# A gated linear unit over 268 MB: two load buffers and two product buffers replaced by three slots with the product packed in place

## The chip, the cores and the metric

The kernel runs on one core of one Trainium2 chip. The metric is the device time of one execution in microseconds (us); lower is better. The time that a run reports is about 2 us more than the span of its profile (936.0 against 933.9 for the profiled run of the kernel before).

## The reference

```python
def setup_inputs():
    return {"x": np.random.randn(8192, 8192).astype(np.float32)}

def reference(x):
    a, b = np.split(x, 2, axis=-1)
    return a * (1 / (1 + np.exp(-b)))
```

Each row of 8192 numbers is cut into halves a and b, and a · sigmoid(b), 4096 numbers, goes out. 268.4 MB are read and 134.2 MB written, all in float32.

## The kernel before

The 8192 rows are cut into 32 tiles. A tile has 128 partitions with two rows each, so 64 KiB per partition come in (one contiguous piece) and 32 KiB go out. SyncE issues the loads, ScalarE does the sigmoid in place and issues the stores, VectorE multiplies into a second tile. Both tiles have two buffers: 2 x (64 + 32) = 192 KiB per partition. (In the cuts of code below, `...` marks what is left out, and some comments after `#` are mine.)

```python
pool = ctx.enter_context(tc.tile_pool(name="io", bufs=2))
for i in range(n_tiles):
    x_sb = pool.tile([P, R * n_cols], fp32)
    o_sb = pool.tile([P, R * half], fp32)
    load = nc.sync.dma_start(out=x_sb, in_=x_t[i])
    ...
    n = 4 if i == n_tiles - 1 else 1        # the last tile in eight small pieces
    w = half // n
    for r in range(R):                      # R = 2 rows
        for c in range(n):
            ...
            nc.scalar.activation(out=b, in_=b, func=SIG)
            nc.vector.tensor_mul(out=o_sb[:, cols], in0=a, in1=b)
            if n > 1:
                nc.scalar.dma_start(out=out_t[i, :, cols], in_=o_sb[:, cols])
    if n == 1:
        nc.scalar.dma_start(out=out_t[i], in_=o_sb)
```

After scheduling, ScalarE's instruction list is, for every tile but the last: two activations, then that tile's store. At the end of the build the first load is moved up into the entry block.

## Time and profile before

| | before |
|---|---|
| median of 6 runs | 936.12 us (935.98 to 937.0) |
| span of the profile | 933.9 us |
| VectorE, ScalarE busy | 280.9, 230.0 us |
| two DMA queues' packets, share of 16 engines' span | 66.5% + 33.3% |

The page's busy shares, queue totals and chain, and the stretches of time, are shown in the prediction below. Two more views matter later. The first is the issue queue of SyncE, which issues the loads (what waited, for what: us in total, times, longest):

```profile
SPq L28 <- DMA x_sb<-in_x_dram: 482.8, 30, 20.8
SPq L28 <- DVE o_sb L39: 374.3, 30, 12.8
```

A load waits for an earlier load (that of its buffer, two tiles back) and then for the product that frees the buffer. It never waits for a store. The second is the page's list of DMA issues (count, KB each, us from issue to landing, the median):

```profile
out_dram<-o_sb ACTq DMA_DIRECT2D x31, 4096.0 KB, 41.7
x_sb<-in_x_dram SPq DMA_DIRECT2D x32, 45.5
```

### The profile page before, as it was taken

The numbers are of one execution on the slowest core, as the hardware profiler recorded it, in microseconds if no ns is written. First come the engines' busy times: TensorE is split into PE (matmuls) and PEld (weight loads), VectorE is DVE, ScalarE is ACT, GpSimd is POOL, SyncE is SP. The second block draws the span as 40 slices with busy tenths as digits, with TensorE's granted clock in tenths as the row PEclk, the third lists the DMA queues.
The fourth block names the chain that finished last, engine by engine and source line by source line (L and its number), as shares of the span: only waits on it lengthen the run. The fifth ranks groups of instructions, "written<-read, shape, count | busy, mean of one in ns | idle before, by whom it ended". The sixth has DMA issues, their size and how long they took to land.

```text
span 933.9 us, 410 instructions
## 1 busy us (share of the span) xinstructions
DVE 280.9 (30%) x70; ACT 230.0 (25%) x71; POOL 0.2 (0%) x4
## 2 busy tenths in 40 slices
DVE  0333321333213333133331333312333123331234
ACT  1313331133311333203332033320233202333023
POOL 0000000000000000000000000000000000000000
DMA  9999999999999999999999999999999999999998
GB/s 404 420 434 431 453 418 429 439 434 449 420 456 404 452 424 427 449 425 451 412 459 410 438 438 425 451 421 452 413 449 421 431 445 443 429 420 453 410 446 362
DMA packets 10226, 402.67 MB, mean 431 GB/s; under 512 B 1136, under 2 KB 1136, under 8 KB 2160
## 3 DMA queue, kind: packets, MB, share of 16 engines
q1 hardware_dynamic: 4608, 268.44, 66.5%
q10 hardware_dynamic: 5616, 134.22, 33.3%
q14 instruction: 2, 0.02, 0.0%
HBM read 268.44 MB, written 134.22 MB: 431 GB/s over the span
## 4 chain that ended last, share of the span: by engine, by line
DMA 78%; DVE 15%; ACT 6%; issue 0%; DVEq 0%; ACTq 0%
DMA x_sb<-in_x_dram 78%; DVE o_sb L39 15%; ACT x_sb L38 6%; DVEq L61 0%; ACTq L41 0%; ACTq L38 0%
## 5 line engine op out<-in xcount | busy, mean ns | idle before, releaser
L39 DVE TENSOR_TENSOR o_sb<-x_sb 128x4096 f32<-128x4096 f32 (+1 forms) x70 | 280.9, 4056 | 647.2 <-ACT x_sb L38 647.2
L38 ACT ACTIVATE x_sb<-x_sb 128x4096 f32<-128x4096 f32 (+1 forms) x70 | 228.7, 3315 | 695.9 <-DMA x_sb<-in_x_dram 691.8
L38 ACT ACT_TABLE_LOAD x1 | 1.3, 1283 | 0.8 <-PEq L85 0.8
L85 POOL MEMSET const-uint8-127<- 128x1 uint8 x1 | 0.1, 103 | 0.0
L85 POOL MEMSET const-bfloat16-1.0<- 128x1 bf16 x1 | 0.1, 102 | 0.0
L85 POOL MEMSET const-float32-0.0<- 128x1 f32 x1 | 0.1, 99 | 0.2 <-issue 0.2
L85 POOL MEMSET const-float32-1.0<- 128x1 f32 x1 | 0.1, 99 | 0.0
## 6 DMA issues: line engine op xcount, KB each, us to landing
out_dram<-o_sb ACTq DMA_DIRECT2D x31, 4096.0 KB, 41.7
out_dram<-o_sb ACTq DMA_DIRECT2D x8, 512.0 KB, 6.2
x_sb<-in_x_dram SPq DMA_DIRECT2D x32, 45.5
```

The lines of the kernel that those rows point to most:

```text
L38: nc.scalar.activation(out=b, in_=b, func=SIG)
L39: nc.vector.tensor_mul(out=o_sb[:, cols], in0=a, in1=b)
L85: nc = _bacc.Bacc("TRN2", target_bir_lowering=False, num_devices=1)
```

## The change

Its intent: use the same 192 KiB as three slots, so that three loads can be under way; write the product into the first half of its own slot; do one activation and one product per tile; and declare away waits that follow from others, so that each instruction keeps one. (`tc.keep_in_program_order` stops the scheduler from moving an instruction in its engine's list.) The core of the diff (blank lines and unchanged parts cut):

```diff
-    pool = ctx.enter_context(tc.tile_pool(name="io", bufs=2))
+    SLOTS = 3
+    pool = ctx.enter_context(tc.tile_pool(name="slots", bufs=1))
+    slots = [pool.tile([P, R * n_cols], fp32, name=f"slot{k}") for k in range(SLOTS)]
+    def implied(later, *earlier):
+        for e in earlier:
+            tc.declare_no_dep(later.ins, e.ins, reason="follows from the wait that is kept")
...
+        rows = slot.rearrange("p (r h m) -> p r h m", r=R, h=2)
+        packed = slot[:, : R * half].rearrange("p (r m) -> p r m", r=R)
+        def load(cols):
+            ins = nc.sync.dma_start(out=slot[:, cols], in_=x_t[i, :, cols])
+            implied(ins, *(e for e in gone if e not in awaited))   # keeps the slot's last stores
...
+        def glu(r, c):
+            sig = nc.scalar.activation(out=rows[:, r, 1, c], in_=rows[:, r, 1, c], func=SIG)
+            mul = nc.vector.tensor_mul(
+                out=packed[:, r, c], in0=rows[:, r, 0, c], in1=rows[:, r, 1, c]
+            )
...
+            if i == n_tiles - 1:
+                tc.keep_in_program_order(sig)
...
+        def store(cols):
+            ins = nc.scalar.dma_start(out=out_t[i, :, cols], in_=slot[:, cols])
...
+        if i < n_tiles - 1:
+            load(slice(0, R * n_cols))
+            glu(slice(0, R), every)
+            n_stores = R if i == n_tiles - 2 else 1
+            w = R * half // n_stores
+            for k in range(n_stores):
+                store(slice(k * w, (k + 1) * w))
+        else:
+            for r in range(R):
+                load(slice(r * n_cols, (r + 1) * n_cols))
+            for r in range(R):
+                halves = [slice(0, half // 2), slice(half // 2, half)]
+                for c in [every] if r == 0 else halves:
+                    glu(slice(r, r + 1), c)
+                store(slice(r * half, (r + 1) * half))
```

The diff doesn't show one thing. Here is how ScalarE's instruction list compares, as built (A n is the activation of tile n, S n its store):

```
before : A0 A0 S0  A1 A1 S1  A2 A2 S2  A3 A3 S3  A4 A4 S4  ...
changed: A0 S0  A1 S1  A2 S2  A3 A4 S3 S4  A5 S5  A6 A7 S6 S7  A8 S8  ... A27 A28 S27 S28 ...
```

From tile 3 on the scheduler puts every third tile's store behind the next tile's activation, nine times in all.

More of the change, by code (lines that the diff above doesn't have):

```diff
@@ L20, in _tiles @@
     out_t = out.rearrange("(n p r) m -> n p (r m)", p=P, r=R)
-    pool = ctx.enter_context(tc.tile_pool(name="io", bufs=2))
-    first = None
-    for i in range(n_tiles):
-        x_sb = pool.tile([P, R * n_cols], fp32)
-        o_sb = pool.tile([P, R * half], fp32)
-        load = nc.sync.dma_start(out=x_sb, in_=x_t[i])
-        first = first or load
-        n = 4 if i == n_tiles - 1 else 1
-        w = half // n
-        for r in range(R):
-            for c in range(n):
-                lo = r * n_cols + c * w
-                a = x_sb[:, lo : lo + w]
-                b = x_sb[:, lo + half : lo + half + w]
-                cols = slice(r * half + c * w, r * half + (c + 1) * w)
-                nc.scalar.activation(out=b, in_=b, func=SIG)
-                nc.vector.tensor_mul(out=o_sb[:, cols], in0=a, in1=b)
-                if n > 1:
-                    nc.scalar.dma_start(out=out_t[i, :, cols], in_=o_sb[:, cols])
-        if n == 1:
-            nc.scalar.dma_start(out=out_t[i], in_=o_sb)
@@ L44, in _tiles @@
-    return first
+    pool = ctx.enter_context(tc.tile_pool(name="slots", bufs=1))
[3 more added lines that the diff above has]
+            tc.declare_no_dep(later.ins, e.ins, reason="follows from the wait that is kept")
+    kinds = ("loads", "sigs", "muls", "stores")
+    history = [{k: [] for k in kinds} for _ in range(SLOTS)]
+    last_stores = [[] for _ in range(SLOTS)]
+    every = slice(0, half)
@@ new lines, in _tiles @@
+    for i in range(n_tiles):
+        slot = slots[i % SLOTS]
+        old = history[i % SLOTS]
+        now = {k: [] for k in kinds}
+        gone = sum(old.values(), [])
+        awaited = last_stores[i % SLOTS]
+        rows = slot.rearrange("p (r h m) -> p r h m", r=R, h=2)
[3 more added lines that the diff above has]
+            implied(ins, *(e for e in gone if e not in awaited))
+            now["loads"].append(ins)
+        def glu(r, c):
[3 more added lines that the diff above has]
+            )
+            implied(sig, *gone)
+            implied(mul, *gone, *now["loads"])
+            if i == n_tiles - 1:
+                tc.keep_in_program_order(sig)
+            now["sigs"].append(sig)
+            now["muls"].append(mul)
+        def store(cols):
+            ins = nc.scalar.dma_start(out=out_t[i, :, cols], in_=slot[:, cols])
+            implied(ins, *(e for e in gone if e not in old["stores"]), *now["loads"], *now["sigs"])
+            now["stores"].append(ins)
+        if i < n_tiles - 1:
[13 more added lines that the diff above has]
+                store(slice(r * half, (r + 1) * half))
+        for k in kinds:
+            old[k] += now[k]
+        last_stores[i % SLOTS] = now["stores"]
@@ L64 @@
     SP = mybir.EngineType.SP
-    at = next(k for k, i in enumerate(body) if i.engine == SP)
+    at = next(k for k, i in enumerate(body) if i.engine == SP and i.opcode == "DMACopy")
     load = body[at]
```

## The prediction

> **What bounds the kernel now.** I read the page from its top (busy shares, slices, DMA queues), then its chain of waits, then stretches of time with their DMA share, then the issue queue's waits, and last single packet records.
>
> ```profile
> span 933.9 us, 410 instructions
> DVE 280.9 (30%) x70; ACT 230.0 (25%) x71; POOL 0.2 (0%) x4
> DMA  9999999999999999999999999999999999999998
> q1 hardware_dynamic: 4608, 268.44, 66.5%
> q10 hardware_dynamic: 5616, 134.22, 33.3%
> HBM read 268.44 MB, written 134.22 MB: 431 GB/s over the span
> DMA 78%; DVE 15%; ACT 6%; issue 0%; DVEq 0%; ACTq 0%
> ```
>
> The two queues' packets (q1 loads, q10 stores) take 66.5% + 33.3% = 99.8% of the time of the 16 DMA engines: 932 of 933.9 us. VectorE and ScalarE are at 30% and 25%. All 402.7 MB have to cross and the change leaves that number alone. The chain of waits seems to say otherwise: it gives 15% to VectorE and 6% to ScalarE. Here is how that chain looks in order of time (start, us, what), for one pair of tiles:
>
> ```profile
> 811.23 45.45 DMA x_sb<-in_x_dram
> 856.67 0.02 issue
> 856.70 0.02 ACTq L38
> 856.71 0.04 issue
> 856.76 3.62 ACT x_sb L38
> 860.38 0.02 issue
> 860.41 8.77 DVE o_sb L39 x2
> 869.18 0.02 issue
> 869.19 45.42 DMA x_sb<-in_x_dram
> ```
>
> It is the loop through one of two load buffers: load 45.45, first activation 3.62, two products 8.77, next load; 57.96 us for two tiles. The reader is to see that 45.45 us is not the price of a load. The first load of the kernel, alone on the engines, lands after 21.9 us. The later ones stand behind another load and share the engines with stores. So I ask whether the engines are idle anywhere (columns: stretch, us, busy VectorE, ScalarE, GpSimd with counts, clock, DMA share, GB/s; a packet counts where it starts):
>
> ```profile
> 0.00:1.00 1.00, 0.00 (x0) 0.22 (x1) 0.20 (x4) 1.00 0.00 0
> 43.00:914.65 871.65, 262.83 (x60) 213.68 (x60) 0.00 (x0) 1.00 1.00 434
> 914.65:931.00 16.35, 9.35 (x8) 7.90 (x8) 0.00 (x0) 1.00 0.98 409
> 931.00:934.00 3.00, 0.00 (x0) 0.00 (x0) 0.00 (x0) 1.00 0.16 63
> ```
>
> Steady state is 1.00 for 872 us. Even after the last load has landed (914.65) stores keep the engines at 0.98. Only the first microsecond and about two at the end are empty. The packet records settle it: a 64 KiB load packet takes 2.418 us (the 10th and 90th percentile are the same), a 32 KiB store packet 1.213, a 4 KiB one 0.159. Each of 16 engines moves 8 partitions, so a tile costs it 8 x (2.418 + 1.213) = 29.05 us. The loop above makes 57.96 / 2 = 28.98, and from 56.12 to 869.19 the chain passes 28 tiles in 813.07 us, 29.04 each. The period is the packets' time; the loop of waits only follows it.
>
> [...] in mid-run each engine's records go load, store, load, store, 3.63 us a pair. [...]
>
> **The change, part by part.**
>
> 1. Slots. Two load buffers of 64 KiB and two product buffers of 32 KiB per partition become three slots of 64 KiB, the same 192 KiB. A load now waits for the store of its slot three tiles earlier to land, in place of the product two tiles earlier. Three loads start at once. In steady state nothing is gained: the engines were never without a packet, so a load issued earlier only stands longer in its queue.
>
> 2. Longer instructions. From 4096 (3608 ns) and 1024 elements (1046 ns) an activation costs 192 + 0.834 N ns, an estimate of 7.02 us for 8192; the product 8.69. Per tile 7.02 against 7.22 and 8.69 against 8.84, some 31 x 0.35 = 11 us less busy time, all of it beside the DMA: worth 0. But within a tile activation and product no longer overlap: landing to store issue goes from 3.62 + 8.77 = 12.4 to 15.8 us. Does the slot loop hold that? With both queues full: load 8 x 3.63 = 29.05, compute 15.8, store 29.05, and about 3 for issue and receipts: 77 us. Three tiles of DMA work are 87.1 us. There are 10 us to spare, so this loop should not bind, and what is to spare is spent standing in a queue.
>
> 3. Order. Comparing the instruction lists, from the fourth tile on every third store stands behind the next tile's activation on ScalarE's queue (activation 3, activation 4, store 3, store 4, activation 5, store 5). That store waits for another load to land plus 7 us. While it waits, that load is in flight by definition, so packets flow. When that load lands, the third slot's load is either already queued (19.3 us of packets alone, more than the 7 us) or its slot's store still is. So the engines run dry only where a store's landing and a load's last packet nearly coincide: then some 1 to 2 us (issue to first packet was 1.0 us at the start). There are nine such groups. I reckon with none to a few: 0 to 2 us.
>
> 4. The removed waits. A wait that is already satisfied costs tens of ns on a sequencer that is idle (0.02 to 0.04 us pieces in the chain). Worth 0.
>
> 5. Final tile. Before: 8 stores of 4 KiB packets, 64 x 0.159 = 10.18 us per engine. After: two stores of 16 KiB packets; between 0.159 and 1.213 linearly one is 0.611 (estimate), 16 x 0.611 = 9.78. The tile before it: 8 x 1.213 = 9.70 becomes 16 x 0.611 = 9.78. The last load as 16 packets of 32 KiB instead of 8 of 64: 16 x 1.213 - 8 x 2.418 = +0.06. Net -0.26 us.
>
> 6. Does the new tail leave a hole? From the landing of the last row: activation of 2048 elements 1.90, two products 2 x 2.29, issue and first packet about 1.3: 7.8 us until the last store's packets. Queued by then: most likely the second half of the tile before (4.9) and the first row's store (4.9), as that tile's stores were issued about 16 us after its load and shared the engines since. 9.8 covers 7.8 by 2 us. If it doesn't, the hole is a few us.
>
> Start: the first load is moved up as before; same. Sum: 936.19 - 0.26 + 0 to 2, middle about 936.0.
>
> **The rivals.**
>
> A. The chain is to be believed: 21% of it is compute, a third slot takes it off the loop, and the kernel becomes faster; at the whole 21% it would be 740 us. Against it: [...] the measured packets sum to 256 x 2.418 + 248 x 1.213 + 10.2 = 930 us per engine. With 1 us ahead and 2 behind, 933 of the 933.9 us are spoken for. This rival can win at most 1 us, so 935.
>
> B. The store order binds: each group leaves a hole of up to 2 us, nine times, so 936 + 18 = 954. For it: the product buffer is gone, so a load now waits for a transfer's landing and not for an engine, and ScalarE issues the store in order behind an activation that waits for a load. Against it: 10 us to spare per loop and the argument in 3.
>
> C. The tail: the second half of the last row is computed with nothing left in the queue, +2 to +5 us, so 938 to 941. For it: the last store is 2.1 MB at once, where before eight small ones started 2.4 us after the landing. Against it: the 9.8 us queued.
>
> D. Packets of another length. Three slots change which addresses are read and written at a time. If HBM took that badly, 2.418 would grow; it has been the same from the first tile to the last, reads alone (first tile) or beside stores, so I don't expect it.
>
> **Range and chances.** The floor is rival A's 935; runs of one kernel lie within 0.4 us. Above, some holes of B and C: 938 covers two or three. So 936.0, from 935.0 to 938.0 in 8 of 10. To be 2% faster (917.5) [...]: 0.3%. To be 2% slower (954.9) B must come in full: 1.5%.
>
> **What would show it.** The DMA share should stay 1.00 in mid-run and the two queues sum to about 99.7%; the time from issue to landing of a load should fall from 45 towards 30 to 38 us and ScalarE's and VectorE's busy time by about 11 us, with no gain in the span: that would be steps 1, 2. Loads waiting for stores in the issue queue's waits are step 1's new wait. For B, the share falls below 1.00 in stretches that repeat every 87 us. For C, it drops in the last 20 us. D shows in the packet records. The prediction is wrong if the span changes by more than 3 us, and a gain above 1 us would mean that packets got shorter.

## The result

The changed kernel takes 942.43 us in the median of 6 runs (941.58 to 945.11), the kernel before 936.12. The ratio is 1.0068, with a 95% interval of 1.0055 to 1.0081. A ratio here is the mean time of one kernel's fast runs over that of the other's fast runs of the same rounds, so it is not quite the ratio of the medians. All these runs count as fast (a run on one core counts as slow when it is over 1.5% above the fastest of its kernel). The changed kernel is 6.3 us slower, and the predicted range ended at 938.

The page of the changed kernel, in its lines that answer to those of before:

```profile
span 940.8 us, 205 instructions
DVE 278.4 (30%) x34; ACT 226.5 (24%) x35; POOL 0.2 (0%) x4
q1 hardware_dynamic: 4752, 268.44, 66.6%
q10 hardware_dynamic: 4896, 134.22, 33.1%
HBM read 268.44 MB, written 134.22 MB: 428 GB/s over the span
DMA slot<-in_x_dram 43%; DMA out_dram<-slot 38%; DVE slot L63 9%; ACT slot L62 8%; DVEq L112 0%; SPq L57 0%
```

The compute engines work a little less, and the queues still fill 99.7% of the span. But the span is longer, so the packets took 0.997 x 940.8 = 938.0 us per engine instead of 0.998 x 933.9 = 932.0, for the same bytes. Next, SyncE's issue queue and the DMA issues:

```profile
SPq L57 <- DMA out_dram<-slot: 871.9, 29, 69.9
out_dram<-slot ACTq DMA_DIRECT2D x30, 4096.0 KB, 35.4
slot<-in_x_dram SPq DMA_DIRECT2D x31, 35.1
```

Now each load waits for a store, and it lands 35 us after issue instead of 45: it stands behind less. The same stretch of time in steady state and the rest (stretch, us, busy VectorE, ScalarE, GpSimd with counts, clock, DMA share, GB/s), first of the kernel before:

```profile
43.00:914.00 871.00, 262.83 (x60) 213.68 (x60) 0.00 (x0) 1.00 1.00 434
914.00:934.00 20.00, 9.35 (x8) 7.90 (x8) 0.00 (x0) 1.00 0.87 362
```

then of the changed kernel:

```profile
43.00:914.00 871.00, 260.77 (x30) 210.41 (x31) 0.00 (x0) 1.00 1.00 431
914.00:941.00 27.00, 8.92 (x3) 6.11 (x3) 0.00 (x0) 1.00 0.83 356
```

The DMA share is 1.00 in both, while the rate fell from 434 to 431 GB/s. A share that counts a packet as busy from its start to its end can't show that some packets last longer; the rate beside it can.

To see which ones, I read the packet records: 64 KiB packets take 2.418 us, 32 KiB 1.213, 16 KiB 0.611 and 4 KiB 0.159, with hardly an exception in the kernel before. Call what a packet takes beyond that its excess. For each profiled run I sum all packet times and divide by 16 engines; the rest is the span less that sum. About 1.0 us lies ahead of the first packet and 1.2 behind the last. That the rest can be less than these two is because successive records on an engine overlap by 3 to 4 ns, about 2 us over the 640 records of each. So only the differences in the rest between kernels count; they are nearly all idle engine time in the last stretch.

| profile of | span | packets at their usual time | excess | rest |
|---|---|---|---|---|
| before | 933.9 | 930.7 | 2.0 | 1.3 |
| changed | 940.8 | 930.4 | 7.5 | 3.0 |

So of 6.9 us, 5.5 are excess, 1.7 are the rest, and the new tail's work gave back 0.3. In the kernel before, practically all excess is at the start (0.7 at the first packets, 1.2 where the first store joins, about 38 us in). In the changed kernel most of it comes in clusters 87 us apart, one per three tiles. Here is one cluster, in chosen lines of ScalarE, VectorE and both issue queues from 377 us (start, us, what, idle before and its releaser):

```profile
377.25 8.69 DVE L63 TENSOR_TENSOR slot<-slot 128x8192 f32<-128x8192 f32 x1 [27.41 <-ACT slot L62]
394.31 7.03 ACT L62 ACTIVATE slot<-slot 128x8192 f32<-128x8192 f32 x1 [17.09 <-DMA slot<-in_x_dram]
394.32 16.12 ACTq L74 DMA_DIRECT2D out_dram<-slot  x2
422.14 7.03 ACT L62 ACTIVATE slot<-slot 128x8192 f32<-128x8192 f32 x1 [20.80 <-DMA slot<-in_x_dram]
423.35 0.33 SPq L57 DMA_DIRECT2D slot<-in_x_dram  x1
```

By their place in time these are tiles 12 to 15. The product of tile 12 is done at 377.25 + 8.69 = 385.94. Its store is issued at 394.32, 8.4 us later, when load 13 has landed and activation 13 has started. By the records, that store lands at 423.33 and load 15, which waits for it, is issued at 423.35. Load 14 had landed at 422.12. So load 15 is issued onto a load queue that has been empty for 1.2 us. The same happens nine times, with stores held for 8.1 to 8.8 us and loads late by 1.2 to 1.3 us (and once more, by 0.2 us and without a held store, at tile 3). The 1.2 us is about one store packet (1.213): store 12 goes out when load 13 has landed, so it and the waiting load 14 take turns on the engines (from 400 to 418 us 78 load and 79 store packets start), and the store has the last turn (load 14 lands at 422.12, the store at 423.33). One engine's packets over that time, put together from the records by matching starts to ends (start us, L load or S store, us):

```
420.36 S 1.213   421.58 S 1.213   422.80 S 1.213   424.01 S 1.213   425.22 S 1.213
426.42 S 1.213   427.63 L 3.116   430.75 S 1.213   431.96 L 2.418   434.37 S 1.213
```

The engine isn't idle: it does stores alone for some 7 us, and then the first load packet takes 3.116 us instead of 2.418. Not every engine shows it: in this group 7 of the 16 do, and in the nine groups together 90 of the 144 first load packets are long by more than 30 ns, the longest at 3.567 us.

### The profile page after: what moved, and what is told of

Its sections match the earlier page's. It is cut to its first block, busy times and chain, and to the rows that moved or that the text cites. A ratio compares the mean times of both kernels' runs of the same rounds, so it can differ in the third digit from the quotient of the medians.

```text
span 940.8 us, 205 instructions
## 1 busy us (share of the span) xinstructions
DVE 278.4 (30%) x34; ACT 226.5 (24%) x35; POOL 0.2 (0%) x4
## 4 chain that ended last, share of the span: by engine, by line
DMA 81%; DVE 9%; ACT 8%; DVEq 0%; issue 0%; SPq 0%
DMA slot<-in_x_dram 43%; DMA out_dram<-slot 38%; DVE slot L63 9%; ACT slot L62 8%; DVEq L112 0%; SPq L57 0%
## 5 line engine op out<-in xcount | busy, mean ns | idle before, releaser
L63 DVE TENSOR_TENSOR slot<-slot 128x8192 f32<-128x8192 f32 (+2 forms) x34 | 278.4, 8190 | 651.0 <-ACT slot L62 651.0
L62 ACT ACTIVATE slot<-slot 128x8192 f32<-128x8192 f32 (+2 forms) x34 | 225.2, 6627 | 699.3 <-DMA slot<-in_x_dram 689.7
## 6 DMA issues: line engine op xcount, KB each, us to landing
slot<-in_x_dram SPq DMA_DIRECT2D x31, 35.1
```

The costliest lines, as they stand in the source:

```text
L62: sig = nc.scalar.activation(out=rows[:, r, 1, c], in_=rows[:, r, 1, c], func=SIG)
L63: mul = nc.vector.tensor_mul(out=packed[:, r, c], in0=rows[:, r, 0, c], in1=rows[:, r, 1, c])
```

## The experiments

The theory (R): the delayed store delays the load that waits for it, the load queue runs empty, and where it fills again packets take longer. Rivals: any load that waits for a store does this, in whatever order (S); the new tail does it (T); later, a late store costs by itself (D). Each run was timed in five rounds against the kernel before unless it says otherwise, and all gave correct results. Excess and rest are those of the one profiled run, which needn't be at the median. The rounds ran on several chips; the kernel before, timed in each of them, had medians of 935.88 to 936.43 us.

### e1_order: the store order undone

```diff
         def load(cols):
...
+            if i == n_tiles - 1:
+                tc.keep_in_program_order(ins)
...
-            if i == n_tiles - 1:
-                tc.keep_in_program_order(sig)
+            tc.keep_in_program_order(sig)
```

> The changed kernel with every store right behind its own product in ScalarE's order, as in the kernel before (the only other difference: the last tile's two loads are pinned in order). Theory R (a load that is issued after the load ahead of it has landed finds the load queue empty, and its first packets take 0.3 to 1.2 us longer on every engine; this happens ten times in the changed kernel, once per group of three tiles, after the delayed store): without the delayed store the issues are evenly spaced, load to landing 31 to 36 us against a period of 29, so few or no loads find the queue empty; packet excess falls from 7.5 to about 2 us and the time to 936.5 to 938 (the tail is still the new one). Rival S (any load that waits for a store, not the order, starves the queue): the queue empties at every tile, the excess is as large or larger, time 942 to 947. Rival T (the tail alone costs it): unchanged, 942.

A first build without the two lines for the last tile's loads was refused before it ran, for a race: the second of these loads has no wait of its own and had moved ahead of another load. (That build left no run on the record.)

Measured: 936.39 us (935.85 to 937.21), ratio to before 1.0003 (0.9991 to 1.0015). Everything else of the change is still there, and together it costs or gains nothing that these runs can tell from zero. The same stretch of time and the queues:

```profile
q1 hardware_dynamic: 4752, 268.44, 66.6%
q10 hardware_dynamic: 4896, 134.22, 33.3%
43.00:914.00 871.00, 265.18 (x31) 212.85 (x31) 0.00 (x0) 1.00 1.00 433
```

And the order of events (start, us, what, idle before and its releaser):

```profile
372.58 8.69 DVE L65 TENSOR_TENSOR slot<-slot 128x8192 f32<-128x8192 f32 x1 [20.14 <-ACT slot L64]
381.31 0.34 ACTq L75 DMA_DIRECT2D out_dram<-slot  x1
394.69 7.03 ACT L64 ACTIVATE slot<-slot 128x8192 f32<-128x8192 f32 x1 [22.14 <-DMA slot<-in_x_dram]
```

The store goes out at 381.31, right when its product ends (381.27), and does not wait for the activation at 394.69. Excess is 3.0 us (7.5 with the delayed stores), the rest 1.3 (3.0). Only the load of tile 3 still finds its queue empty. Rivals S and T fall: loads still wait for stores, the tail is the new one.

### e2_newtail: the new tail on the kernel before

```diff
-        load = nc.sync.dma_start(out=x_sb, in_=x_t[i])
+        for k in range(loads):                     # two halves for the last tile
+            part = slice(k * R * n_cols // loads, (k + 1) * R * n_cols // loads)
+            load = nc.sync.dma_start(out=x_sb[:, part], in_=x_t[i, :, part])
...
+            if last:
+                cols = slice(r * half, (r + 1) * half)
+                nc.scalar.dma_start(out=out_t[i, :, cols], in_=o_sb[:, cols])
...                                                # two stores for the tile before it
```

> The kernel before with the new tail alone: last load in two halves, two stores for each of the last two tiles, last row in two halves. Theory R plus a hole in the tail: 1.3 us of the loss belong to the tail (the engines' idle time at the end was 0.9 us before and 2.6 after, work is 0.3 less), so 937 to 938. Prediction's step 5: 0.26 us faster, 935.9. Rival T: all of the 6.3 us, 942.

Measured: 936.06 us against 936.04, ratio 0.9997 (0.9985 to 1.0010). The tail costs nothing by itself, so my own expectation of 937 to 938 was wrong: the 1.7 us that the changed kernel loses in the last stretch come with the delayed stores, not with the tail (e1_order, with the same tail, doesn't have them either). Whether it gains the predicted 0.26 us is below what this resolves. The profiled run, the slowest of the five (936.71), has an excess of 2.1 us and a rest of 2.2, so 0.9 us more idle time at the end than in the kernel before; no such loss shows in the median.

### e3_dose: nine loads held in the kernel before

```diff
+        held = i >= 4 and i % 3 == 1 and i < n_tiles - 1
+        if held:
+            # slot of tile i-2 is touched after tile i-1 has landed: load i waits for that
+            older = nc.vector.tensor_copy(out=tiles[-2][:, 0:1], in_=tiles[-1][:, 0:1])
         load = nc.sync.dma_start(out=x_sb, in_=x_t[i])
```

> The kernel before with nothing else changed than that nine of its loads, every third, are held until the load ahead of them has landed (a one-element copy that reads that tile writes the slot). Two buffers, old store order, old tail. Theory R: nine restarts of an empty load queue, 0.3 to 0.6 us each on every engine, seen as longer first load packets: 936.1 + 3 to 5 = 939 to 941, engines not idle in between as stores are queued. Rival (an emptied queue costs nothing as long as the other has packets; the loss comes from the in-place slots or the tail): 936 to 936.5.

Measured: 941.88 us (940.38 to 944.57), ratio 1.0066 (1.0052 to 1.0081), a little more than expected. Nine loads were issued 0.31 us after the load ahead had landed; the excess is 5.7 us and the rest 2.6. So holding loads alone, with two buffers and the old tail, costs about as much as the whole change did (the store queue then ran dry too). But the expectation was wrong in where it would stand. The long packets are mostly not the load's first ones. They are the load packet just ahead of the first store packet, when the store queue, which had drained meanwhile, got work again (109 of 171 packets in that place are long by more than 30 ns, those 109 by 0.36 us in the mean).

### e5_early: the loads taken off the late store

The packed product covers only the first half of a slot, so the second row can be loaded as soon as the product is done.

```diff
-            implied(ins, *(e for e in gone if e not in awaited))
+            kept = awaited if cols.start == 0 else old["muls"][-1:]
+            implied(ins, *(e for e in gone if e not in kept))
+            tc.keep_in_program_order(ins)
...
-            load(slice(0, R * n_cols))
+            load(slice(n_cols, R * n_cols))
+            load(slice(0, n_cols))
```

(the last tile's two loads change places too)

> The changed kernel with each load in two halves by rows: the second row of a slot, which the packed product does not touch, is loaded once the product is done, the first row once the store has landed. Store order still paired, tail unchanged. Loads now have 32 KiB packets: 512 x 1.213 against 256 x 2.418 us, about 2 us more work per engine. Theory R: the load queue always holds half a tile more, no load finds it empty, the restart excess of 5 us goes: 942.4 - 5 + 2 = 938.5 to 940. Rivals S and T: the excess stays, 944 to 945.

Measured: 946.93 us in the median, in two groups: 941.8, 942.5, 942.9 and 951.0, 951.4, 951.7. The ratio is 1.0116 (1.0080 to 1.0151). The profiled run is of the lower group. In it no load finds its queue empty and the excess is 2.1 us, as theory R says, although the store order is still the paired one and the store queue ran empty 22 times. The smaller load packets cost 2.3 us, also as expected. What wasn't expected is the last stretch:

```profile
43.00:914.00 871.00, 260.78 (x30) 209.10 (x30) 0.00 (x0) 1.00 1.00 433
914.00:940.00 26.00, 8.92 (x3) 7.33 (x3) 0.00 (x0) 1.00 0.70 299
```

The engines are at 0.70 there, and the rest is 5.3 us. So the steady state is healed and the time isn't, as a hole at the end takes its place: even the lower group is above the 938.5 to 940 expected. The load packets are also half as long here, and no run tells whether the excess went because of the early issue or because of that. The upper group has no profile.

### e6_half: the delayed stores only from tile 15 on

```diff
-            tc.keep_in_program_order(sig)
+            if i < 16 or i == n_tiles - 1:
+                tc.keep_in_program_order(sig)
```

(against e1_order; the scheduler then pairs five of the nine groups)

> The changed kernel with the paired store order only from tile 15 on: five of the nine groups. If each group's delayed store costs its own share: 936.4 + 5/9 of 6.0 = 939.5 to 940, five loads issued onto an empty queue beside the first, packet excess 3.0 + 5/9 x 4.5 = 5.5 us. If the loss comes once (in the end or in how the first group leaves the queues): 942, or 936.5.

Measured: 939.97 us (938.27 to 943.28), ratio 1.0039 (1.0025 to 1.0053); the time is as expected. Five loads besides that of tile 3 were issued onto an empty queue, 1.2 us late each, and no others. The excess is 4.1 us, less than the 5.5 expected, and the rest is 2.6. But this profile is of a run of 938.82 us, 1.1 below the median, so it doesn't settle how the loss is shared out.

### e7_late: the same delayed stores in the kernel before

```diff
+            if late and r == R - 1:
+                tile, sb = late.pop()
+                tc.keep_in_program_order(nc.scalar.dma_start(out=out_t[tile], in_=sb))
+        if n == 1 and i % 3 == 0 and 3 <= i < n_tiles - 2:
+            late.append((i, o_sb))
```

(the activations are pinned in order, and the other stores too)

> The kernel before with the same delayed stores (the store of tiles 3, 6, ... 27 behind the next tile's activations, nine times), two buffers and product tiles as before. There no load waits for a store. Theory R (the delayed store costs because a load waits for it and the load queue runs empty): the loads keep two deep, no load finds its queue empty, no packet excess from it: 936 to 937. Rival D (a late store costs by itself, as the store queue runs dry and refills): nine dry store queues, 939 to 942. The held-load run leaves this open: there the longer packets stood at the refilling of the store queue.

Measured: 952.64 us (949.34 to 955.51), ratio 1.0168 (1.0148 to 1.0187). It was meant to show that a late store is harmless where no load waits for it directly; it costs 16 us instead, more than in the changed kernel. Rival D is right in that a late store can do harm without a load that waits for it, but not by the way it named. What waits here, in the view of all waits, is the product, for the earlier store of its buffer, and what suffers is the end:

```profile
DVE o_sb L41 <- DMA out_dram<-o_sb: 331.1, 16, 21.5
920.00:953.00 33.00, 9.80 (x8) 8.45 (x8) 0.00 (x0) 1.00 0.58 243
```

The engines are at 0.58 in the last 33 us (rest 11.9 us). The excess is 10.1 us, and it stands around every tile's change of transfers, with neither queue ever empty up to the landing of its last packet, save once. So long packets don't need an empty queue of loads, and theory R isn't a general rule for them.

### e8_first: a version that might have beaten both

```diff
+            early = i == SLOTS and cols.start > 0
+            kept = old["muls"][-1:] if early else awaited
...
+            parts = [(n_cols, R * n_cols), (0, n_cols)] if i == SLOTS else [(0, R * n_cols)]
+            for part in parts:
+                load(slice(*part))
```

(against e1_order: tile 3 is loaded in two halves)

> A version that might beat both: the store order restored, and the first reload of a slot (tile 3) in two halves, the second row as soon as the product is done, as that load still found its queue empty in the restored order and the packets around it took 1.34 us longer. Theory R: that cluster goes, 936.4 - 1.3 = 935.1, packet excess 1.6 to 1.7 us. If the long packets there belong to something else: 936.4.

Measured: 936.63 us (936.34 to 939.41), ratio 1.0008 (0.9996 to 1.0020): no gain. The cluster at tile 3 is gone, and one of 1.5 us stands 89 us later, where a load is now issued 0.19 us after the one ahead has landed. The gap was only moved. (The profile is of the slowest of these runs, 939.41.)

### e5b_early: the early second rows once more

> The early second rows once more, for a second profile: its runs fell into two groups, at 942 and 951, and the first profile was of the lower. No theory for the upper; if it comes up, its packet excess and idle engine time tell whether packets got longer or the tail hole did.

One look, on another chip, of unknown state as single runs are: 942.07 us, again the lower group, excess 2.6 us, rest 5.1. It confirms the first profile and leaves the upper group unseen.

### e9_more: thirteen delayed stores

```diff
+            if i % 2 == 1 and 3 <= i < n_tiles - 3:
+                late.append((i, slot, gone, old, now))
+            else:
                 for k in range(n_stores):
                     store(slice(k * w, (k + 1) * w))
```

(against e1_order; a tile in `late` is stored after the next tile's activation)

> More of the same dose: the changed kernel with thirteen delayed stores (tiles 3, 5, ... 27, each behind the next tile's activation) in place of nine. The runs so far: none 936.4, five 940.0, nine 942.4, so 0.67 us each. If each costs its own share: 936.4 + 13 x 0.67 = 945. If the rhythm of three (the delayed store always that of the same slot) matters and not the number: anything else, most likely 942 or less.

Measured: 946.46 us (944.65 to 948.80), ratio 1.0112 (1.0099 to 1.0126); 945 was expected. Thirteen loads besides that of tile 3 were issued 1.2 us late. The rhythm of three isn't needed. The dose isn't quite the same, though: most stores were held for about 15 us here, against 8.1 to 8.8 in the changed kernel. Together (times are medians, excess and rest of the profiled runs):

| delayed stores | 0 (e1_order) | 5 (e6_half) | 9 (changed) | 13 (e9_more) |
|---|---|---|---|---|
| time, us | 936.4 | 940.0 | 942.4 | 946.5 |
| excess, us | 3.0 | 4.1 | 7.5 | 10.4 |
| rest, us | 1.3 | 2.6 | 3.0 | 3.9 |

Per delayed store that is 3.6 / 5 = 0.72, 6.0 / 9 = 0.67 and 10.1 / 13 = 0.77 us.

### e10_both: early second rows with the store order restored

```diff
-            if i == n_tiles - 1:
-                tc.keep_in_program_order(sig)
+            tc.keep_in_program_order(sig)
```

(against e5_early)

> The early second rows together with the restored store order. In the early-row runs the long packets were gone (excess 2.0 to 2.4 us) but the engines stood idle 5.8 us in the last stretch. If that hole comes from the paired order at the end (two activations and two products in a row before the last stores), it goes here: nominal work 932.6 + excess 2 + 1 at the start + 2 at the end: span 937.6, time 939.7. If it comes from the loads having run ahead of the stores: it stays, 942 or more. No two groups of times (942 and 951) if those come from the order.

Measured: two groups again, 941.1 and 941.9 beside 950.4 to 955.5; the ratio of the fast runs is 1.0124 (1.0083 to 1.0165). The two groups come with the early second rows, whatever the order. The lower group is 1.4 to 2.2 us above the 939.7 expected, so restoring the order did not bring the gain hoped for; no profile of that group shows whether the hole at the end is still there. Why there are two groups stays open.

## Why the prediction was wrong

**Where it failed.** It is step 3, the order: "I reckon with none to a few: 0 to 2 us." That term measured 942.43 - 936.39 = 6.0 us. I had seen the reordered stores in the instruction lists and had listed the full cost as rival B, but sized it by one kind of loss only, engines that run dry. Its announced sign, a share below 1.00 every 87 us, didn't come (0.99 to 1.01 in all 87 us stretches). The step argued that "packets flow", and they do. What it missed is that flowing packets can take longer: of the 6.2 us between the spans of the two profiles (940.8 and 934.6), 4.5 are excess (7.5 against 3.0) and 1.7 the rest, in the last stretch (3.0 against 1.3).

The same step had one fact wrong on the way. It let the store wait for the next load "plus 7 us", as if for the activation to end. The store was issued 0.01 us after the activation, 7.03 us long, had started. The delay was 8.4 us, the wait for the load alone. And the 1.0 us from issue to first packet was read at the start, on empty engines. Behind queued stores the first load packet came 3.5 to 4.3 us after the issue in the nine groups.

**Step 2's margin.** "There are 10 us to spare" was worked out for a store issued as soon as its product is done, and e1_order agrees: there the loop doesn't bind. (The "about 3 for issue and receipts" in its sum is an estimate: in the kernel before, the first load has its first packet 1.0 us after its issue and lands 0.4 us after its last packet ends; counted once for the load and once for the store, 2.8.) In the changed kernel 8.4 of the 10 us go to the delay, and what was left did not keep a second load queued: from load 12 to load 15, in the same slot, the loop took 34.9 (load) + 15.8 (compute) + 8.4 (delay) + 29.0 (store) = 88.1 us, where three tiles of packets take 87.1. The load alone took 5.9 us more than its 29.05. Both steps used the margin without taking one from the other. The busy time that this step promised, 11 us, was 2.5 + 3.5 = 6.0: I had added single durations, where successive instructions overlap a little (a pair of activations occupied 7.12 us, not 7.22). It was off the path, so it made no difference.

**Rival D.** It said that longer packets would come from addresses and that I didn't expect them. Packets did get longer, but the same three slots at the same addresses have none of it after tile 3 in e1_order (excess 3.0 us in all, against 7.5). It is the timing of the issues.

**What held.** That three slots, fewer and longer instructions, the removed waits and the new tail are together worth about nothing: e1_order has all of them at a ratio of 1.0003. The 8.69 us estimated for the longer product was measured at 8.69 (the products of the kernel before, 1.221 us for 1024 elements and 4.422 for 4096, give 8.69 for 8192 on a straight line). That the chain's 21% of compute can't be had (rival A). Load to landing at 30 to 38 us: 35.1. Loads waiting for stores: 871.9 us. That the tail leaves no hole (step 6, rival C): true of e1_order, and in time of e2_newtail, not of the changed kernel, where the delayed stores change what is queued at the end. And "what would show it" named the right record, the packets' duration, for the wrong rival.

**What is shown and what isn't.** Shown: the delayed stores cost it, by undoing them (e1_order) and by dose (0, 5, 9, 13). Shown too: each delayed store makes one load find its queue empty (1.2 to 1.3 us after the load ahead has landed), and in e5_early, where half of each load doesn't depend on the store, the excess goes from 7.5 to 2.1 us. But the packets are smaller there, so that the empty load queue is what makes the packets long is likely and not shown. Not shown either: why a packet takes longer at such a place. In e3_dose the long packets stand at the return of the stores, in e7_late around every change of transfers, and in the changed kernel the store queue also ran empty nine times, for 7 us each, with 0.05 us of excess in all within 9 us of the nine issues that filled it again. Evenly fed queues, each with more than one transfer, are the state in which practically none appeared (0.1 us after the first 60 us in the kernel before; the whole excess is 2.0 us there, 2.1 in e2_newtail, and 3.0 in e1_order with tile 3); I have no rule for the rest.

No version beat the kernel before. Its packets at their usual time need 930.7 of 933.9 us, so less than 4 us were left to win by rearranging. The 0.3% that the prediction gave to 917.5 us was an estimate of mine: it would have needed packets shorter than 2.418 and 1.213 us.

## What to carry to other kernels

When a kernel is bound by DMA, as this one is (99.8% of the span), check after each change that every load and every store is issued well before the one ahead of it on its queue lands (12 to 17 us before in the faster kernel here; not enough by itself, as e7_late shows), and read the rate beside the busy share: with the engines at 1.00 in both, this rate fell from 434 to 431 GB/s. Look at the scheduled order of each engine's list, not only at the program: here a DMA issue stood in line for 8.4 us behind an activation that waited for another load. And when sizing a delay, subtract it from the slack of the loop that it lies in before calling it hidden.
